# Query weights by head, five late heads, two streaming buffers and seven kept places in a four-layer decoder trunk

## The chip, the cores and the metric

The kernel runs on one core of a Trainium2 chip. The metric is the device time of one execution in microseconds, as the median of several runs. One further execution was taken with the hardware profiler; all views below are of that one.

## The reference, cut to what matters

The program is a decoder trunk of four layers over 256 tokens of 1024 numbers, all in float32. Each layer has a token mixer (HGRN2, FoX attention, Mamba-2 SSD, HGRN2 again) and then a PEER feed-forward: eight heads each choose 16 of 16384 experts for every token, and an expert is one row of a table `u` and one of a table `v`.

```python
for i in range(DEPTH):                      # 4 layers
    hn = rmsnorm(h, norm_mix[i])
    h = h + mixer_i(hn)                     # HGRN2, FoX, SSD, HGRN2
    h = h + peer_ffn(rmsnorm(h, norm_ffn[i]), peer_w_q[i], peer_keys[i], peer_u[i], peer_v[i])
return rmsnorm(h, norm_final)

def peer_ffn(h, w_q, sub_keys, u_tab, v_tab):
    q = (xb @ w_q).reshape(M, 8, 2, 128)                 # w_q: 1024 x 2048
    s = jnp.einsum('mhcd,hckd->mhck', q, sub_keys)       # 2 x 128 scores a head
    sv, si = lax.top_k(s, 16)
    # the 16 x 16 sums of both halves, their top 16, softmax over these: idx, gates
    u, v = u_tab[idx], v_tab[idx]                        # 8 x 16 rows of each a token
    act = gelu(einsum('md,mhkd->mhk', xb, u)) * gates
    return einsum('mhk,mhkd->md', act, v)
```

## The kernel before, in words

**Stages, pairs and gathers.** The 256 tokens are two tiles of 128. A stage is the PEER part of one layer for one tile, so there are eight: stages 0, 2, 4 and 6 (the first, third, fifth and seventh) are first tiles, the others second tiles. A stage has eight heads, a head eight pairs, a pair two gathers. A gather is one indirect DMA on POOL's queue that brings 128 expert rows, u and v side by side, 1 MB in all, into a buffer of the `ring`. For each pair DVE makes two dot products (`dot`), ACT the gate (`active`), PE adds the weighted v rows to `acc` (`spread`, four products of 64x512), and then both buffers go back to the ring. The ring has seven buffers (`GB`), and further 1 MB places are lent to it while they are empty (`given_back`).

**Work beside the pairs.** While stage s is worked off, `side(s)` prepares stage s + 1: its mixer, its norms and its query scores. It is a Python generator; the loop at the end of the program takes one step of it a pair or so, so that a running cost follows `SIDE[s]`, and takes all that is left at pair 62. `Plan` lays out a mixer's work by numbered slots (`pe` for products, `at` for the other engines), and `hold(n, r)` keeps slot n back until r heads are routed. The order on every engine is fixed when the program is built.

**Routing.** `route` takes the scores of one head from `SS` and makes indices (`ix`, the cast from `gs` is its last step on DVE) and gates; heads are routed in order, up to four ahead of the one being gathered. `route_first` makes the very first head's indices in two halves, so that five gathers can go out early.

**Weights.** All weights but the expert tables come as units of 128 x 2048 numbers, 1 MB, on SP's queue. `stream` lists the units in the order of use, and `loads` issues them in `order` as places come free; where the next one has no place, all behind it wait. There are four kinds of places. A streaming buffer (`raw`, `NRAW` of them) is free again when its unit is used. A kept place (`spots`, `NKEPT` of them) holds a mixer unit from the first tile's use to the second's, so that it comes in once for both; `KEEP` gives for each weight the units that have a place, in the places' order. (For FoX one more unit is kept in the mixer's scratch space.) `homes` are other spaces lent to single units of the program's first stretch. `"rest"`, `"x"` and `"keys"` in `order` are other loads, and `"factors"`, `"heads"` and `"states"` are points that must be passed before what follows is loaded.

**Queries.** The query weights of a layer are eight units. Before, two units together held 512 columns, which are two heads. `queries` makes a first tile's heads 0 to 3 at the end of the stage ahead and a second tile's heads 0 to 7: the products are 512 wide (tokens are the stationary side), ACT evicts them to `QB`, PE turns them, ACT copies the turn to `QT`, PE multiplies it with the keys, and ACT copies the scores to `SS`. A first tile's heads 4 to 7 come later, inside its own stage, in the slots of the second tile's mixer (`late_queries`): there the weights are the stationary side and the products, 128 wide, come out turned already. Their units are `tails`, put into the stream behind mixer units by `TAIL`, and kept for the second tile. `alone` makes the program's first two heads one by one.

Of the kernel before, what the change touches and what calls it, by code (L numbers as in the profile page):

```python
# [11 lines left out]
F32 = mybir.dt.float32  # L12
# [19 lines left out]
NRAW = 3  # L32
# [12 lines left out]
SIDE = (47, 31, 43.5, 100, 100, 35.2, 45, 1.8)  # L45
# [55 lines left out]

def _cols(v):
    return np.ascontiguousarray(v.reshape(-1, P).T)
# [12 lines left out]
def _layout(x, norm_mix, norm_ffn, norm_final, hgrn_lb_logits, hgrn_w_in, hgrn_gnorm, hgrn_w_out,  # L116
# [18 lines left out]
    for i in range(DEPTH):  # L135
        a["wq%d" % i] = _in_units(peer_w_q[i])
# [35 lines left out]
def trunk(ctx: ExitStack, tc: tile.TileContext, d: dict, out: bass.AP):  # L172
# [113 lines left out]
    order += range(35, len(stream))  # L286
# [45 lines left out]
    def loads():  # L332

        while order:
# [12 lines left out]
            else:  # L347
# [9 lines left out]
                elif u in homes:  # L357
                    r = homes[u]
                elif pos[0] < NRAW:
                    pos[0] += 1  # L360
                    r = rawp.tile([P, UNIT], F32, name="raw")
                else:
                    return
                if u == 0:
                    for e in (slice(0, HALF), slice(HALF, UNIT)):
                        nc.sync.dma_start(r[:, e], d[nm][i][:, e])
# [4 lines left out]
                raws[u] = r, keep or u in homes  # L371
# [7 lines left out]
    def half(nm, use):  # L379
# [3 lines left out]
        use(raws[u][0].rearrange("p (k c n) -> p k c n", k=2, c=2)[:, k])  # L383
        pos[1] += 1
        if k:
            r, stays = raws.pop(u)
# [170 lines left out]
    def hgrn(l, t, carry):  # L557
# [204 lines left out]
        if t:  # L762
            late_queries(p, l, 4, 9)
# [47 lines left out]
    def fox(l, t, carry):  # L811
# [99 lines left out]
        if t:  # L911
            late_queries(p, l, 4, 9)
# [5 lines left out]
    def ssd(l, t, carry):  # L918
# [228 lines left out]
        if t:  # L1147
            late_queries(p, l, 4, 9)
# [12 lines left out]
    def place_of(s, hh):  # L1161

        return hh if s % 2 or hh not in (4, 5) else hh - 4

    def late_queries(p, l, *starts):

        s = 2 * l
        root = 1.0 if s else rts[1][:, 2:3]
        bs = {}

        def products(g, n):
            if n == 0:
                bs[g] = pjp.tile([P, 512], F32, name="pj")
            ws = [raws[tails[l, 2 * g + i]][0].rearrange("p (k n) -> p k n", k=4) for i in range(2)]
            for k in range(DC):
                mm(bs[g][:, n * P:(n + 1) * P], ws[k // 4][:, k % 4, n * P:(n + 1) * P], xA[:, k], k == 0, k == DC - 1)
            if n == 3:
                for i in range(2):
                    raws.pop(tails[l, 2 * g + i])

        def turned_queries(g):
            return at_["SS"][:, (g - 1) * 512:g * 512].rearrange("p (g t) -> p g t", g=4)

        def evac(g):
            assert routed[0] >= 8 * s + 4, (s, g, routed)
            nc.scalar.copy(turned_queries(g), bs.pop(g).rearrange("p (g t) -> p g t", g=4))

        def score(g):
            b, qt = bank(), turned_queries(g)
            for i in range(4):  # L1190
                mm(b[:, i * P:(i + 1) * P], qt[:, i], keys[:, 4 * g + i], True, True)

            def use():
                h0 = place_of(s, 2 * g)
# [507 lines left out]
```

## Time and profile before

| what | before |
|---|---|
| median of 3 runs | 3159.31 us (3158.54 to 3159.74) |
| profiled execution, time | 3157.22 us |
| profiled execution, span from the first to the last instruction | 3155.5 us |
| busy: PE, DVE, ACT, POOL | 82%, 67%, 49%, 39% |
| moved by DMA | 1292.65 MB, mean 410 GB/s |
| gathers | 1028 DMAs on POOL's queue |
| first gather issued | 109.43 us |

The rows of the profile name an engine, the line of the program (often that of a helper: L249 is any product, L253 a turn, L224 an activation, L211 any DVE operation), the operation and its tiles as out<-in. A float32 product of the program is two rows of PE in the profile, called passes here; a turn is one. In a timeline the first two numbers are the start and the length in us, and what stands in brackets is the idle time ahead and what ended it. In a table of groups the count follows the x, then the busy time in us, the mean ns of one, and the idle time. Most tiles are parts of one large tile, `arena`; `raw`, `pj`, `ps` and `acc` are tiles of their own (`ps` and `pj` are both PSUM banks).

### The profile page before, as it was taken

The numbers are of one execution on the slowest core, as the hardware profiler recorded it, in microseconds if no ns is written. First come the engines' busy times: TensorE is split into PE (matmuls) and PEld (weight loads), VectorE is DVE, ScalarE is ACT, GpSimd is POOL, SyncE is SP. The second block draws the span as 40 slices with busy tenths as digits, with TensorE's granted clock in tenths as the row PEclk, the third lists the DMA queues.
The fourth block names the chain that finished last, engine by engine and source line by source line (L and its number), as shares of the span: only waits on it lengthen the run. The fifth ranks groups of instructions, "written<-read, shape, count | busy, mean of one in ns | idle before, by whom it ended". The sixth has DMA issues, their size and how long they took to land.

```text
span 3155.5 us, 31905 instructions
## 1 busy us (share of the span) xinstructions
PE 2600.9 (82%) x8970; PEld 998.7 (32%) x8970; DVE 2111.5 (67%) x5602; ACT 1546.5 (49%) x4406; POOL 1222.5 (39%) x1034
## 2 busy tenths in 40 slices
PE   9798887787789886999878998778877888876666
PEld 4333332232234432344223443222322333321111
DVE  1666758575666856878476885586656766687755
ACT  3455435374344743577344784355443555344433
POOL 0234434344433533433343333343344433345454
PEclk9999998999899998999989999899989999999999
DMA  8799999999999999999999999999999999999998
GB/s 327 302 421 421 420 421 420 416 401 421 419 414 418 421 421 421 418 400 411 415 421 411 404 419 422 420 419 416 410 414 418 412 421 410 421 421 421 421 421 336
DMA packets 179198, 1292.65 MB, mean 410 GB/s; under 512 B 19920, under 2 KB 20432, under 8 KB 22352
## 3 DMA queue, kind: packets, MB, share of 16 engines
q0 software_dynamic: 147776, 1073.81, 82.4%
q1 hardware_dynamic: 31248, 216.82, 16.7%
q8 instruction: 74, 1.21, 0.2%
q14 instruction: 100, 0.82, 0.1%
HBM read 1289.49 MB, written 1.05 MB: 409 GB/s over the span
## 4 chain that ended last, share of the span: by engine, by line
DMA 52%; DVE 14%; issue 14%; PE 8%; POOL 4%; ACT 2%; POOLq 0%; DVEq 0%; ACTq 0%
DMA arena<-in_uv,ix 52%; DVE arena L211 9%; POOL arena L1462 4%; PE acc L1530 4%; PE pj L249 3%; PE ps L249 2%; DVE eq L211 1%; ACT L224 1%; DVE af L211 1%; ACT dg L224 1%; ACT arena L224 0%; DVE gs L211 0%; DVE si L211 0%; DVE ti L211 0%; PE ps L253 0%
## 5 line engine op out<-in xcount | busy, mean ns | idle before, releaser
L1462 POOL DMA_INDIRECT arena<-in_uv,ix x1028 | 1220.4, 1187 | 1915.9 <-PE acc L1530 1128.6
L211 DVE SCALAR_TENSOR_TENSOR arena<-arena 128x1024 f32<-128x1024 f32 (+3 forms) x1280 | 1317.4, 1048 | 867.4 <-DMA arena<-in_uv,ix 857.6
L1530 PE MATMUL acc<-arena,dg 128*64 128x512 f32 x4096 | 1432.1, 667 | 527.1 <-ACT dg L224 524.5
L224 ACT ACTIVATE dots<-dots 128x1 f32<-128x1 f32 x1024 | 203.6, 199 | 1354.0 <-DVE arena L211 1353.4
L1530 PEld LDWEIGHTS acc<-arena,dg 128*64 128x64 f32 x4096 | 350.3, 145 | 1427.3 <-ACT dg L224 1029.2
L249 PE MATMUL pj<-raw,arena 128*128 128x512 f32 x1184 | 555.1, 610 | 4.9 <-DMA raw<-in_ssm 2.3
L224 ACT ACT_TABLE_LOAD x328 | 420.8, 1283 | 7.6 <-DVE fst L211 1.3
L224 ACT ACTIVATE dg<-dg,dots 128x64 f32<-128x64 f32 x1024 | 356.1, 348 | 33.2
L249 PE MATMUL pj<-arena 128*128 128x512 f32 (+2 forms) x1136 | 347.1, 455 | 4.8 <-ACT arena L976 1.8
L249 PEld LDWEIGHTS pj<-raw,arena 128*128 128x128 f32 x1184 | 215.2, 192 | 343.2 <-issue 320.2
L224 ACT ACTIVATE dg<-m,gs 128x64 f32<-128x64 f32 x1024 | 293.8, 335 | 0.0
L249 PEld LDWEIGHTS pj<-arena 128*128 128x128 f32 x1136 | 174.4, 193 | 181.8 <-issue 163.6
L249 PE MATMUL ps<-arena 128*128 128x128 f32 (+3 forms) x992 | 130.7, 284 | 1.5 <-ACT arena L1260 1.0
L249 PEld LDWEIGHTS ps<-arena 128*128 128x128 f32 (+2 forms) x992 | 100.8, 166 | 66.5 <-issue 38.4
L253 PE MATMUL ps<-fst,arena 128*128 128x128 f32 x536 | 83.9, 282 | 7.2 <-DVE arena L211 4.9
L224 ACT ACTIVATE arena<-arena 128x512 f32<-128x512 f32 (+3 forms) x132 | 67.7, 555 | 43.6 <-DVE arena L211 41.2
L253 PEld LDWEIGHTS ps<-fst,arena 128*128 128x128 f32 x536 | 61.3, 143 | 78.5 <-issue 43.9
L211 DVE DVE_READ_ACCUMULATOR arena<-arena 128x1 f32 x1024 | 84.6, 83 | 0.0
L211 DVE FIND_INDEX8 si<-sv,arena 128x8 uint32<-128x128 f32 x256 | 69.8, 285 | 0.0
L249 PE MATMUL ps<-cst,arena 128*128 128x128 f32 (+3 forms) x288 | 66.6, 358 | 0.1
L211 DVE MAX8 sv<-arena 128x8 f32<-128x128 f32 x256 | 61.6, 282 | 3.5 <-ACT arena L1264 3.4
L224 ACT ACTIVATE arena<-ps 128x512 f32<-128x512 f32 (+4 forms) x120 | 46.7, 435 | 25.4 <-PE ps L249 24.7
(130 smaller groups left out, 1246.1 us busy)
## 6 DMA issues: line engine op xcount, KB each, us to landing
raw<-in_ssm SPq DMA_DIRECT2D x52, 1024.0 KB, 9.5
raw<-in_hg SPq DMA_DIRECT2D x50, 1024.0 KB, 9.5
raw<-in_wq SPq DMA_DIRECT2D x28, 1024.0 KB, 9.4
arena<-in_wq SPq DMA_DIRECT2D x20, 1024.0 KB, 9.2
raw<-in_fox SPq DMA_DIRECT2D x18, 1024.0 KB, 9.2
arena<-in_hg SPq DMA_DIRECT2D x17, 1024.0 KB, 13.4
arena<-in_uv,ix POOLq DMA_INDIRECT x1028, 16.4
arena<-in_fox SPq DMA_DIRECT2D x7, 1024.0 KB, 13.8
```

What stands on the lines that cost most here:

```text
L211: return getattr(nc.vector, name)(o, *a, **k)
L224: nc.scalar.activation(o, i, f, **k)
L249: nc.tensor.matmul(o, w, m, start=start, stop=stop)
L253: nc.tensor.transpose(o, i, ident)
L1462: nc.gpsimd.indirect_dma_start(o, None, src, bass.IndirectOffsetOnAxis(ap=ix, axis=0))
L1530: nc.tensor.matmul(accs[s][e][g * 64:g * 64 + 64], dg[:, g], v, start=hh == 0 and q == 0, stop=hh == 7 and q == NQ - 1)
```

## The change

The query weights are laid out by head: a unit is the 256 columns of one head for all 1024 rows. All query products are made in turned form, 128 wide with the weights stationary, so that no turn is left. A first tile's heads 0 to 2 are made ahead of its stage (`AHEAD_HEADS`), heads 3 to 7 inside it, one in every second slot from slot 2 on. There are two streaming buffers for three, and seven kept places for six. More units of the first stretch have homes, and the orders, holds and two of the pacing numbers are adjusted.

```diff
-NRAW = 3
+NRAW = 2
-KEEP = {"hg": (0, 1, 4, 6, 12, 17), "fox": (0, 1, 4, 6, 9, 13, 11), "ssm": (0, 1, 4, 6, 15, 24), "wq": (4, 5, 6, 7)}
-TAIL = ((6, 4), (6, 5), (8, 6), (9, 7))
-NKEPT = 6
+KEEP = {"hg": (0, 1, 2, 4, 6, 11, 16), "fox": (0, 1, 2, 4, 6, 9, 13, 11), "ssm": (0, 1, 2, 4, 6, 14, 24), "wq": (3, 4, 5, 6, 7)}
+TAIL = ((5, 3), (5, 4), (7, 5), (8, 6), (9, 7))
+AHEAD_HEADS = 3
+NKEPT = 7
-SIDE = (47, 31, 43.5, 100, 100, 35.2, 45, 1.8)
+SIDE = (47, 31, 45, 100, 100, 35.2, 46, 1.8)
+def _head_units(w):
+    k, n = w.shape
+    a = w.reshape(k // P, P, n // 256, 256).transpose(2, 1, 0, 3)
+    return np.ascontiguousarray(a).reshape(n // 256, P, UNIT)
-        a["wq%d" % i] = _in_units(peer_w_q[i])
+        a["wq%d" % i] = _head_units(peer_w_q[i])
-            stream += [("wq%d" % l, i) for i in range(8 if t else 4)]
+            stream += [("wq%d" % l, i) for i in range(8 if t else AHEAD_HEADS)]
-    homes = {4: GB[0], 16: GB[0], 18: GB[1], 19: GB[2], 20: GB[3], 21: GB[4], 22: GB[5], 23: GB[6],
-             26: mix[:, SPACE:SPACE + UNIT], 27: mix[:, D:3 * D], 29: mix[:, 3 * D:5 * D]}
-    order = [0, 1, 2, "rest", *range(3, 10), 22, 10, 11, 12, 23, 13, 14, 15, 16, "x", 17, 20, 18, 21, 19, "keys",
-             "factors", 24, 25, 26, "heads", 27, 28, "states", 29, 30, 33, 34, 31, 32]
+    homes = {3: GB[0], 5: GB[1], 7: GB[2], 8: GB[3], 9: GB[4], 10: at_["XR"], 12: at_["SS"], 15: GB[0], 17: GB[1], 18: GB[2], 19: GB[3], 20: GB[4], 21: GB[5], 22: GB[6],
+             28: mix[:, SPACE:SPACE + UNIT], 26: mix[:, D:3 * D], 32: mix[:, 3 * D:5 * D]}
+    order = [0, 1, 2, "rest", *range(3, 14), 22, 14, 15, 16, 17, "x", 18, 19, 20, 21, "keys",
+             "factors", 23, 24, 25, 28, 27, "heads", 26, 31, "states", 32, 34, 36, 29, 30, 33, 35, 37]
-            late_queries(p, l, 4, 9)
+            late_queries(p, l, (2, 4, 6, 8, 10))
...
+    def free_at(s, hh):
+        if s % 2:
+            return 8 * (s - 1) + (5, 6, 7, 7, 7, 7, 7, 8)[hh]
+        return 8 * s + hh - 2 if hh >= AHEAD_HEADS else 8 * s
+    def head_products(b, ws, x):
+        for n in range(2):
+            for k in range(DC):
+                mm(b[:, n * P:(n + 1) * P], ws[k // 4][:, k % 4, n * P:(n + 1) * P], x[:, k], k == 0, k == DC - 1)
+    def turned_queries(o, b):
+        nc.scalar.copy(o, b[:, 0:256].rearrange("p (c t) -> p c t", c=2))
     def late_queries(p, l, slots):
         s = 2 * l
+        for hh, n in zip(range(AHEAD_HEADS, 8), slots):
+            qt = SS[:, (0, 1, 2, 3, 6)[hh - 3]]
+            def products(hh=hh, qt=qt):
+                b = bank()
+                head_products(b, [r.rearrange("p (c n) -> p c n", n=256) for r in raws.pop(tails[l, hh])[0]], xA)
+                later(lambda: turned_queries(qt, b))
+            p.hold(n, free_at(s, hh))
+            p.pe(n, products)
+            p.pe(n + 1, score, s, hh, qt)
...
+        for n, hh in enumerate(range(0 if s else 2, 8 if s % 2 else AHEAD_HEADS)):
+            p.pe(n, products, hh)
+            p.at(n, lambda hh=hh: turned_queries(QT[hh % 2], bs.pop(hh)))
+            p.hold(n + 1, free_at(s, hh))
+            p.pe(n + 1, score, s, hh, QT[hh % 2])
+        yield from p.run(99)
```

`score` now scales the program's first scores as ACT copies them to `SS`, where the eviction to `QB` did it before; `alone` makes its two heads in the same turned form, into two banks with a copy each.

PE's rows around the program's first score, before (`ps<-fst,arena` 128x128 are turns, 64x128 is the spreading of the first tile's tokens for the dot products):

```order
L249 MATMUL pj<-arena 128x512 x2
L249 MATMUL pj<-arena 128x256 x2
L253 MATMUL ps<-fst,arena 128x128 x4
L249 MATMUL pj<-arena 128x256 x6
L253 MATMUL ps<-fst,arena 128x128 x2
L249 MATMUL ps<-arena 128x128 x2
L249 MATMUL pj<-arena 128x256 x8
L249 MATMUL ps<-fst,arena 64x128 x32
```

And after:

```order
L256 MATMUL pj<-arena 128x512 x2
L256 MATMUL ps<-arena 128x128 x4
L260 MATMUL ps<-fst,arena 128x128 x4
L256 MATMUL ps<-arena 128x128 x30
L256 MATMUL ps<-fst,arena 64x128 x32
L256 MATMUL ps<-arena 128x128 x2
L256 MATMUL pj<-arena 128x128 x16
```

The eight products of 256 columns for each of the first two heads have become sixteen of 128 (the run of 30 is the rest of the first head's, its two score products and the second head's), and the turn of two ahead of the score is gone.

PE's rows in stage 0 at the first late heads, before (`acc<-arena,dg` 64x512 x4 is one pair, `pj<-arena` 128x512 x4 a unit of the second tile's mixer, `pj<-arena` 128x128 the late query products):

```order
L249 MATMUL pj<-arena 128x128 x16
L1530 MATMUL acc<-arena,dg 64x512 x4
L249 MATMUL pj<-arena 128x512 x4
L1530 MATMUL acc<-arena,dg 64x512 x4
L249 MATMUL ps<-cst,arena 128x512 x2
L249 MATMUL pj<-arena 128x128 x8
```

And after, where they are `ps<-arena` 128x128 x16:

```order
L256 MATMUL pj<-arena 128x512 x4
L1528 MATMUL acc<-arena,dg 64x512 x4
L256 MATMUL ps<-arena 128x128 x16
L1528 MATMUL acc<-arena,dg 64x512 x4
L256 MATMUL pj<-arena 128x512 x4
L1528 MATMUL acc<-arena,dg 64x512 x4
L256 MATMUL ps<-arena 128x128 x2
```

The two scores of a late head (the x2) now follow its products after one mixer unit; before, four heads came as two groups, each made over several pairs and scored together.

SP's rows at the end of stage 0, where the second tile's queries and then the next layer's first units are loaded, before:

```order
L368 DMA raw<-in_hg 128x2048 x8
L368 DMA raw<-in_wq 128x2048 x4
L368 DMA arena<-in_fox 128x2048 x2
L368 DMA raw<-in_fox 128x2048 x2
L368 DMA arena<-in_fox 128x2048
```

And after:

```order
L378 DMA raw<-in_hg 128x2048 x8
L378 DMA raw<-in_wq 128x2048 x3
L378 DMA arena<-in_fox 128x2048 x3
L378 DMA raw<-in_fox 128x2048
L378 DMA arena<-in_fox 128x2048
```

One query unit fewer is loaded, since five of the eight are kept, and three of FoX's first four units go to kept places for two.

More of the change, by code (lines that the diff above doesn't have):

```diff
@@ L1161, in place_of @@
     def place_of(s, hh):
-        return hh if s % 2 or hh not in (4, 5) else hh - 4
-    def late_queries(p, l, *starts):
-        s = 2 * l
[L1168 to L1194, printed above, removed]
-                act(SS[:, h0:h0 + 2], b.rearrange("p (h c k) -> p h c k", h=2, c=2), AF.Copy, scale=root)
-                scored.update((s, 2 * g + i) for i in range(2))
-            later(use)
-        for g, n in zip((2, 3), starts):
-            for i in range(4):
-                p.pe(n + i // 2, products, g, i)
-            if g == 2:
-                p.hold(n, 8 * s + 4)
-            p.at(n + 1, evac, g)
-            p.pe(n + 2, score, g)
@@ new lines, in place_of, with score, use @@
+        return hh if s % 2 or hh not in (4, 5, 6) else hh - 4
+    def free_at(s, hh):
+        if s % 2:
+            return 8 * (s - 1) + (5, 6, 7, 7, 7, 7, 7, 8)[hh]
+        return 8 * s + hh - 2 if hh >= AHEAD_HEADS else 8 * s
+    def score(s, hh, qt):
+        assert routed[0] >= free_at(s, hh), (s, hh, routed)
+        b = bank()
+        for c in range(2):
+            mm(b[:, c * P:(c + 1) * P], qt[:, c], keys[:, 2 * hh + c], True, True)
+        def use():
+            act(SS[:, place_of(s, hh)], b[:, 0:256].rearrange("p (c k) -> p c k", c=2), AF.Copy,
+                scale=1.0 if s else rts[1][:, 2:3])
+            scored.add((s, hh))
+        later(use)
@@ L1210, in queries @@
         x = xT if s % 2 else xA
-        ub = {}
+        bs = {}
         top[0] = FREE[KIND[l]]
-        QB = al(512)
-        QT = al(512).rearrange("p (g t) -> p g t", g=4)
-        root = 1.0 if s else rts[1][:, 2:3]
-        def evac(g):
-            act(QB, ub.pop(g), AF.Copy, scale=root)
-        def turns(g):
-            turned(QB, lambda b: nc.scalar.copy(QT, b))
-        def score(g):
-            assert s == 0 or routed[0] >= min(8 * s, 8 * s - 6 + 2 * g + 4 * (s % 2)), (s, g, routed)
-            b = bank()
-            for i in range(4):
-                mm(b[:, i * P:(i + 1) * P], QT[:, i], keys[:, 4 * g + i], True, True)
-            def use():
-                nc.scalar.copy(SS[:, 2 * g:2 * g + 2], b.rearrange("p (h c k) -> p h c k", h=2, c=2))
-                scored.update((s, 2 * g + i) for i in range(2))
-            later(use)
+        QT = [al(256).rearrange("p (c t) -> p c t", c=2) for _ in range(2)]
@@ L1271, in queries @@
         p = Plan()
-        gs = range(0 if s else 1, 4 if s % 2 else 2)
-        p.halves(range(2 * len(gs)), project("wq%d" % l, ub, gs, x))
-        for i, g in enumerate(gs):
-            p.at(2 * i + 1, evac, g)
-            p.pe(2 * i + 2, turns, g)
-            p.pe(2 * i + 3, score, g)
-        for n, _ in enumerate(p.run(99)):
-            yield
-            while n % 2 and s and routed[0] < min(8 * s, 8 * s - 6 + 4 * (s % 2) + len([1 for k in scored if k[0] == s])):
-                yield "wait"
+        for n, hh in enumerate(range(0 if s else 2, 8 if s % 2 else AHEAD_HEADS)):
[4 more added lines that the diff above has]
+        yield from p.run(99)
     def top16(chains):
@@ L1404, in route_first @@
         got[0, 0] = ix, gs
-        while ring[0] is not homes[22]:
+        while ring[0] is not homes[21]:
             fetch(sent[0])
@@ L1601, in trunk @@
         next(first)
+    next(first)
     lone[0] = False
@@ L1608, in trunk @@
         next(first)
+    next(first)
     next(routing)
     next(first)
-    while pos[1] < 2 * 24:
+    while pos[1] < 2 * 23:
         next(first)
```

69 lines of the change are left out of this document (42 added, 27 removed).

## The prediction

> **What bounds the kernel now.** I read the page's summary of engines and slices first, then the queues, then windows along the span, then the waits.
>
> ```profile
> span 3155.5 us, 31905 instructions
> PE 2600.9 (82%) x8970; PEld 998.7 (32%) x8970; DVE 2111.5 (67%) x5602; ACT 1546.5 (49%) x4406; POOL 1222.5 (39%) x1034
> ...
> DMA  8799999999999999999999999999999999999998
> ...
> q0 software_dynamic: 147776, 1073.81, 82.4%
> q1 hardware_dynamic: 31248, 216.82, 16.7%
> ```
>
> No compute engine is full, and the DMA digit is 9 in every one of the 40 slices but the first two and the last. The two queues' shares add up to 99.1% of the 16 engines' span: q0 carries the expert rows (gathers on POOL's queue), q1 the weights (SP's queue). In the window view the last two columns are the DMA share and GB/s:
>
> ```profile
> 0.00:90.00 90.00, 86.73 (x284) 43.12 (x285) 18.75 (x43) 29.00 (x50) 1.16 (x5) 1.00 0.84 335
> 90.00:110.00 20.00, 18.92 (x109) 12.62 (x109) 8.59 (x40) 5.62 (x12) 0.57 (x1) 1.00 0.05 21
> 200.00:300.00 100.00, 91.31 (x376) 41.22 (x376) 62.27 (x161) 54.99 (x147) 40.82 (x33) 0.98 1.01 421
> 1410.00:1420.00 10.00, 10.00 (x39) 3.81 (x38) 9.05 (x31) 3.63 (x11) 4.34 (x3) 1.00 0.80 291
> 1490.00:1500.00 10.00, 10.00 (x33) 4.35 (x33) 9.66 (x20) 5.39 (x16) 2.63 (x3) 1.00 0.85 336
> 1510.00:1530.00 20.00, 20.00 (x57) 6.91 (x55) 4.93 (x8) 3.27 (x13) 5.63 (x6) 1.00 1.01 422
> 1770.00:1780.00 10.00, 10.00 (x49) 6.04 (x49) 8.59 (x32) 9.78 (x27) 3.78 (x4) 1.00 0.90 338
> 120.00:3130.00 3010.00, 2471.72 (x8501) 934.74 (x8501) 2062.46 (x5467) 1496.26 (x4304) 1208.99 (x1019) 0.93 1.01 417
> ```
>
> The program has two parts. Up to about 110 us PE is the bound (86.73 of 90 us busy) and DMA falls idle at the end, 0.05 in 90 to 110. From 120 to 3130 us DMA is the bound: 417 GB/s on average against 421 in an undisturbed window. The difference is (1 - 417/421) x 3010 = 28.6 us of lost transfer, and it lies in dips such as 1410, 1490 and 1770, where PE shows 10.00 of 10 us. One more view agrees: POOL, which issues the gathers, waits for buffers to be released, not for numbers, and a load takes far longer to land than its bytes need:
>
> ```profile
> POOL arena L1462 <- PE acc L1530: 1128.6, 387, 8.7
> ...
> raw<-in_ssm SPq DMA_DIRECT2D x52, 1024.0 KB, 9.5
> raw<-in_wq SPq DMA_DIRECT2D x28, 1024.0 KB, 9.4
> ...
> arena<-in_uv,ix POOLq DMA_INDIRECT x1028, 16.4
> ```
>
> So in the second part a byte not moved is worth its transfer time: one unit of 1,048,576 bytes at 421 GB/s is **2.49 us**. (q1's own row gives 0.167 x 3155.5 / 216.82 MB, or 2.55 us for a unit.)
>
> **Part 1: fewer unit loads.** Counting the load rows of both programs, 199 units come in before (148 into streaming buffers, the rest into kept places and lent space) and 191 after: in each of four layers one more mixer unit is kept, the first tile's queries at the stage's end load three units for four, the late ones five for four, the second tile's three for four. What counts is which are behind the first gather.
>
> ```profile
> 73.79 49.23 SPq L368 DMA_DIRECT2D arena<-in_hg  x3
> 123.07 0.90 SPq L368 DMA_DIRECT2D raw<-in_hg  x2
> 109.43 1.09 POOL L1462 DMA_INDIRECT arena<-in_uv,ix  x1 [107.74 <-DVE ix L211]
> ```
>
> The load list blocks at "states", which is freed after the first gathers (the third load of the merged row is that one, at 123 us). Ahead of it stand 24 units of the first tile and two of the second, 26 in all; in the changed list 23 and two, 25. So 173 follow before and 166 after: **seven** units are saved where DMA is the bound, 7 x 2.49 = **17.4 us** (17.9 by q1's row). The eighth is saved where DMA has idle time, and counts nothing; if PE waited for loads there, it would be a gain too, but PE's 86.73 of 90 excludes more than 3 us.
>
> **Part 2: the first route.** The second part begins when the first gather is issued, so PE's path up to the first score counts in full.
>
> ```profile
> 98.94 2.94 PE L249 MATMUL pj<-arena 128*128 128x256 f32 x12
> 101.92 0.47 ACT L224 ACTIVATE arena<-pj,rts 128x256 f32<-128x256 f32 x1 [1.69 <-PE pj L249]
> 102.44 0.44 PE L253 MATMUL ps<-fst,arena 128*128 128x128 f32 x2 [0.56 <-ACT arena L224]
> 102.97 0.37 ACT L1260 COPY arena<-ps 128x256 f32<-128x256 f32 x1 [0.58 <-PE ps L253]
> 103.40 0.71 PE L249 MATMUL ps<-arena 128*128 128x128 f32 x4 [0.52 <-ACT arena L1260]
> 201.90 3.84 PE L249 MATMUL pj<-arena 128*128 128x128 f32 x32
> ...
> L892 ACT COPY arena<-ps 128x128 f32<-128x128 f32 x16 | 4.0, 248 | 0.0
> L249 PE MATMUL pj<-arena 128*128 128x512 f32 x592 | 277.2, 612 | 4.8 <-ACT arena L976 1.8 <-DVE arena L211 1.4 <-DMA arena<-in_hg 0.9
> L249 PE MATMUL pj<-arena 128*128 128x128 f32 x512 | 62.5, 278 | 0.0
> ```
>
> Before: products, one eviction of 0.47 us, a turn, a copy, then the score at 103.40. After: products, two copies of 128x128 (2 x 0.25 us), then the score: the stretch from 102.44 to 103.40, 0.96 us, goes. The products themselves are 32 passes 128 wide for 16 passes 256 wide: by the row at 201.90 (32 such passes, the late queries before) 3.84 us, against 16/12 x 2.94 = 3.92 us. Bounds: 1.04 us of gain (0.96 and the 0.08 of the passes); none, if the hand-overs between the two copies and the score cost what the turn did. I take **0.9 us**. Loads cannot delay this path: the first 15 units have a place that waits for no other unit, where three streaming buffers were refilled after use, so they only come earlier.
>
> **Part 3: queries in turned form, later on.** A head costs 32 passes 128 wide, 32 x 62.5/512 = 3.91 us, for 8 passes 512 wide, 8 x 277.2/592 = 3.75 us, less two turns (0.44 by the row at 102.44). 48 heads change their form, 12 a layer: from 48 x (3.91 - 3.75 - 0.44), 13 us less of PE, to 48 x 0.16, 8 us more, if the turns hid. PE is 82% busy beside a full DMA, which covers it: **0**; without that cover it would be these 13 or 8 us, and both ends stay in the range. ACT's evictions per head become two of 256 columns; ACT is 49% busy: nothing.
>
> **Part 4: five late heads for four.** In the order, the fourth head of a first tile is routed (its index cast on DVE) after 17 pairs of its stage in the first and third stages, 14 and 16 in the fifth and seventh, and first needed for pair 24: a lead of 7 pairs at the least. Before, the fifth head of the first stage was routed after 25 pairs for pair 32, also 7 (only the program's second head leads by less, 3 pairs in both). In time that was, from the cast to the first gather,
>
> ```profile
> 267.18 0.17 DVE L211 CAST ix<-gs 128x16 int32<-128x16 f32 x1
> 290.62 0.17 DVE L211 CAST ix<-gs 128x16 int32<-128x16 f32 x1
> 295.12 0.94 POOL L1462 DMA_INDIRECT arena<-in_uv,ix  x1 [0.31 <-PE ps L249]
> ```
>
> 28 us (267.18 to 295.12). The queue of gathers does not run dry for it: 0. The new holds in the late slots wait for heads that are routed by then; the old one at 8s + 4 goes.
>
> **Part 5: two streaming buffers.** A unit's load now waits for the unit two before it, not three. Where units come 10 us and more apart that is harmless. The tightest place is the Mamba output projection at the end of a stage:
>
> ```profile
> 1509.17 1.95 PE L249 MATMUL pj<-raw,arena 128*128 128x512 f32 x4 [0.85 <-DMA raw<-in_ssm]
> 1518.27 1.94 PE L1530 MATMUL acc<-arena,dg 128*64 128x512 f32 x8
> 1520.13 3.70 PE L249 MATMUL pj<-raw,arena 128*128 128x512 f32 x8
> 1525.63 3.70 PE L249 MATMUL pj<-raw,arena 128*128 128x512 f32 x8
> ```
>
> There PE takes a unit each 5.5 us (1520.13 to 1525.63: a unit 3.70, a pair 1.94). With two buffers a buffer's cycle is 9.5 us to land and 3.7 to use, 13.2 us for two units, 6.6 each: 1.1 us late for each of about seven units, twice, 15 us; and in each of seven bursts of query units the third is issued 2 x 5.5 - 3.7 = 7.3 us before its use and lands after 9.4, 2.1 us late, 15 us again. That is 30 us of PE waiting, if all of it showed. But a pair with its unit needs 3 x 2.49 = 7.5 us of DMA, more than 6.6: DMA is the bound in these bursts too (0.85 of wait already shows while 1510 to 1530 runs at 422 GB/s), and seven gather buffers hold 17.4 us. Bounds: 0 and 30 us; I take **0**, nearest the row of 422, and let a rival take more.
>
> **Sum.** 17.4 + 0.9 = 18.3 us. The profiled execution took 3157.2 us (span 3155.5), so 3138.9; it stood 2.1 us under the median of the runs, 3159.3, so **3141 us**.
>
> **The rivals.** (a) The dips grow: PE's work stays while DMA's shrinks, and the two-buffer waits fall where PE is already full (1410, 1490, 1770). A fifth to two fifths of part 5's 30 us comes back: 3147 to 3153. For it: three dips lie in the Mamba stages. Against: the 422 GB/s in the burst itself.
> (b) The dips shrink: the late heads stand on alternate slots, not on neighbouring ones (1770 is such a place), and one head leaves the forced end of three stages. A sixth to a third of 28.6 us: 3131 to 3136.
> (c) Slower: the fourth head's route comes late, since its unit lands in a place that the stage's first unit frees two slots earlier. The 28 us of lead must go first, then 18.3 + 6.3 us over four stages, 6.2 each: it decides from 34 us on. A slip of two routes, 23.4 us each from the cast at 267.18 to the next, would cost 4 x (46.8 - 28) = 75 us: 3216. Against: every lead in the order is 7 pairs or more.
> (d) Slower: a 128-wide pass waits for its own weight load. The load's row is
>
> ```profile
> L249 PEld LDWEIGHTS pj<-raw,arena 128*128 128x128 f32 x1184 | 215.2, 192 | 343.2 <-issue 320.2
> ```
>
> 192 ns; not hidden, a pass would take 0.122 + 0.192 = 0.314 us, a head 10.0, a pair with it 12.0 us against DMA's 7.5. It decides from 5.6 us a head on. 41 heads in bursts (11 a layer, less three ahead of the gathers) x 4.5 = 185 us, less seven bursts' cover of 17.4: 3204. Against: the row of 62.5 us for 512 such passes has the loads in it.
> The Trainium skill, "TensorE: Matmul & The Clock Gate", section "Back-to-back issue gap", speaks for (d): it says that a stream of weight load and matmul pairs is paced by both, about 81 ns at 128 columns and 131 at 512. By that ratio a head would cost 4 x 81/131 = 2.5 times as much, an estimate of 9.3 us. The trace disagrees for this kernel's float32 passes: 0.122 against 0.469 us, a ratio of 3.8 for four times the columns.
> (e) The change does not do what it says: excluded for the loads, which are rows of the program; only their place could differ, and then the time would be the same within what a measurement can tell, 0.2% or 6.3 us.
>
> **Chances.** Forecast, 3136 to 3146: 0.62. (a) 0.18, a third of it not faster by 0.2%. (b) 0.11. (c) 0.04. (d) 0.03. (e) 0.02. Faster by over 0.2% (under 3153): 0.62 + 0.11 + 0.12 = 0.85; within: 0.06 + 0.02 = 0.08; slower: 0.07. The range takes in (b) and most of (a): 3130 to 3152.
>
> **What the changed profile would show.** Part 1: q1 down from 216.82 by 8.4 to 208.4 MB, q0 as it was, and 120 to 3110 us again near 417 GB/s. Part 2: the first gather near 108.5 us. Part 3: about 0.12 us a pass in the 128-wide rows. Part 4: gaps on POOL waiting for the index cast would show it wrong. Part 5: PE waiting for raw rises from a few us to some 20, without a fall of GB/s at the ends of the Mamba stages; lower GB/s there is (a). I am wrong if the mean of 417 falls by more than 1 GB/s.

## The result, and the profile after

The changed kernel takes **3141.07 us** (median of four runs, 3137.26 to 3144.13) against 3159.52 us (3158.54 to 3159.88) before on the same chip: a ratio of 0.9941, 95% interval 0.9924 to 0.9959, or 18.45 us less. The forecast was 3141.0. Its profiled execution took 3143.29 us, 2.2 us over its median, where that of before stood 2.3 us under its own; so the two traces differ by 14 us only, and a second profiled execution of the changed kernel (below) is read beside the first.

The page of the changed kernel: span, engines, the slices' DMA digits, the two queues, and two rows of the tables.

```profile
span 3141.5 us, 34004 instructions
PE 2593.9 (83%) x10010; PEld 1094.9 (35%) x10010; DVE 2111.1 (67%) x5602; ACT 1544.5 (49%) x4449; POOL 1224.8 (39%) x1034
...
DMA  8699999999999999999999999999999999999998
...
q0 software_dynamic: 147776, 1073.81, 82.7%
q1 hardware_dynamic: 30096, 208.43, 16.1%
```

q0 is what it was; q1 is down from 216.82 to 208.43 MB, eight units of 1.0486 MB. The engines' work is the same to a part in two hundred, but for PE's weight loads (PEld, 1094.9 us for 998.7). DMA is still full from the third slice on.

Windows of the changed kernel (start:end and length, busy time and rows of PE, PEld, DVE, ACT and POOL, granted clock, DMA share, GB/s): the whole second part, the stretches in which before had its dips of 1410 and 1770, the two Mamba output projections, and the fourth, fifth and sixth stages. A stage begins 8 or 9 us earlier than before, so the stretches of the dips are 8 us earlier too.

```profile
120.00:3110.00 2990.00, 2461.15 (x9489) 1025.23 (x9488) 2059.92 (x5462) 1493.28 (x4341) 1209.27 (x1017) 0.93 1.01 416
1378.00:1418.00 40.00, 37.61 (x137) 15.75 (x136) 32.52 (x99) 30.58 (x75) 11.93 (x10) 1.00 0.99 405
1757.00:1787.00 30.00, 26.54 (x120) 14.08 (x121) 25.50 (x79) 23.27 (x60) 11.38 (x10) 1.00 1.01 421
1480.00:1540.00 60.00, 48.82 (x136) 17.95 (x134) 30.07 (x58) 22.58 (x66) 17.58 (x16) 0.91 0.90 351
1910.00:1960.00 50.00, 42.20 (x118) 15.53 (x117) 21.76 (x40) 14.46 (x47) 11.19 (x12) 0.90 0.97 388
1226.00:1636.00 410.00, 342.41 (x1246) 139.95 (x1246) 303.71 (x838) 241.93 (x641) 151.44 (x128) 0.93 0.99 408
1636.00:2057.00 421.00, 373.11 (x1621) 183.77 (x1622) 295.65 (x796) 235.55 (x642) 151.71 (x128) 0.94 1.01 416
2057.00:2427.00 370.00, 302.35 (x1020) 108.42 (x1018) 255.15 (x658) 180.13 (x521) 148.41 (x130) 0.92 1.01 419
```

The same stretches of before that the prediction did not show:

```profile
1386.00:1426.00 40.00, 39.19 (x151) 17.65 (x150) 32.59 (x98) 30.92 (x78) 15.08 (x11) 1.00 0.95 382
1765.00:1795.00 30.00, 28.37 (x139) 15.89 (x139) 28.35 (x85) 26.25 (x62) 10.43 (x9) 1.00 0.97 379
1480.00:1540.00 60.00, 50.94 (x154) 18.67 (x154) 34.40 (x75) 22.84 (x65) 16.24 (x16) 0.98 0.98 402
1910.00:1960.00 50.00, 42.22 (x109) 13.31 (x109) 23.30 (x48) 19.26 (x58) 14.99 (x15) 0.90 1.01 421
1235.00:1644.00 409.00, 349.04 (x1195) 135.91 (x1194) 300.90 (x828) 239.95 (x639) 153.22 (x128) 0.95 1.00 413
1644.00:2062.00 418.00, 370.58 (x1404) 161.21 (x1402) 294.48 (x801) 233.54 (x622) 150.43 (x129) 0.94 1.01 416
2062.00:2440.00 378.00, 303.96 (x972) 104.63 (x970) 251.65 (x636) 179.97 (x520) 154.18 (x129) 0.92 1.01 415
```

The mean of the second part is 416 GB/s, where it was 417. But it is made up otherwise. The dip around 1410 is smaller (405 GB/s over its 40 us for 382), that around 1770 is gone from its 30 us (421 for 379). The two Mamba output projections, 1480 to 1540 and 1910 to 1960, fell from 402 to 351 and from 421 to 388. The sixth stage rose from 415 to 419. The engines' totals tell nothing of this, the GB/s by stage do; so the experiments are read by one measure: **lost transfer**, (1 - GB/s / 421.5) x length of a stage, with the GB/s unrounded and 421.5 as the undisturbed rate. For the fourth stage it is (1 - 408/421.5) x 410, or 13 us, after, and (1 - 413/421.5) x 409, or 8 us, before. "All eight" in the table is 120 to 3110 us. The measure is good to some 3 us in the sum: where two executions differ by it, their spans agree with it to that much in most cases (one is 4.5 us off).

### The profile page after: what moved, and what is told of

Its sections match the earlier page's. It is cut to its first block, busy times and chain, and to the rows that moved or that the text cites. A ratio compares the mean times of both kernels' runs of the same rounds, so it can differ in the third digit from the quotient of the medians.

```text
span 3141.5 us, 34004 instructions
## 1 busy us (share of the span) xinstructions
PE 2593.9 (83%) x10010; PEld 1094.9 (35%) x10010; DVE 2111.1 (67%) x5602; ACT 1544.5 (49%) x4449; POOL 1224.8 (39%) x1034
## 3 DMA queue, kind: packets, MB, share of 16 engines
q1 hardware_dynamic: 30096, 208.43, 16.1%
## 4 chain that ended last, share of the span: by engine, by line
DMA 48%; issue 15%; PE 13%; DVE 10%; POOL 5%; ACT 3%; POOLq 0%; DVEq 0%
DMA arena<-in_uv,ix 46%; DVE arena L218 7%; PE acc L1528 5%; POOL arena L1460 5%; PE pj L256 5%; PE ps L256 3%; DMA raw<-in_ssm 1%; ACT L231 1%; DVE eq L218 1%; ACT dg L231 1%; DVE af L218 1%; ACT arena L231 1%; PE ps L260 0%; DVE gs L218 0%; DMA raw<-in_wq 0%
## 5 line engine op out<-in xcount | busy, mean ns | idle before, releaser
L256 PE MATMUL pj<-raw,arena 128*128 128x512 f32 x832 | 400.5, 623 | 26.4 <-DMA raw<-in_ssm 22.9
L231 ACT ACTIVATE dg<-dg,dots 128x64 f32<-128x64 f32 x1024 | 356.1, 348 | 33.2
L256 PE MATMUL pj<-arena 128*128 128x128 f32 (+1 forms) x1248 | 344.3, 428 | 2.1 <-DVE arena L218 1.0
L256 PEld LDWEIGHTS pj<-raw,arena 128*128 128x128 f32 x832 | 154.0, 196 | 272.0 <-issue 234.2
L256 PE MATMUL ps<-arena 128*128 128x128 f32 (+5 forms) x1696 | 224.9, 284 | 4.3 <-ACT arena L1267 4.3
L256 PEld LDWEIGHTS ps<-arena 128*128 128x128 f32 (+3 forms) x1696 | 184.7, 177 | 106.2 <-issue 58.4
L256 PE MATMUL pj<-arena,raw 128*128 128x128 f32 x672 | 81.3, 280 | 4.9 <-DMA raw<-in_wq 4.9
L231 ACT ACTIVATE arena<-ps 128x256 f32<-128x256 f32 (+3 forms) x170 | 63.9, 407 | 41.8 <-PE ps L256 41.1
L256 PEld LDWEIGHTS pj<-arena,raw 128*128 128x128 f32 x672 | 78.6, 196 | 11.3 <-DVE arena L218 5.7
L260 PE MATMUL ps<-fst,arena 128*128 128x128 f32 x440 | 69.8, 286 | 2.4 <-DVE arena L218 2.2
```

Of the source, the lines that this page charges most:

```text
L231: nc.scalar.activation(o, i, f, **k)
L256: nc.tensor.matmul(o, w, m, start=start, stop=stop)
L260: nc.tensor.transpose(o, i, ident)
```

## Experiments

Every kernel was timed against the kernel before on the same chip, in turns, and profiled once. Their lost transfer, in us:

| kernel | 4th stage | 5th | 6th | 4th to 6th | all eight | first gather at |
|---|---|---|---|---|---|---|
| before | 8.0 | 5.9 | 5.4 | 19.3 | 32.6 | 109.43 |
| changed | 13.4 | 5.4 | 2.3 | 21.1 | 36.6 | 107.69 |
| changed, second time | 12.2 | 5.5 | 2.0 | 19.7 | 32.6 | 107.38 |
| three streaming buffers, six kept | 7.4 | 4.5 | 6.0 | 17.9 | 30.1 | 108.46 |
| old queries, two and seven | 13.4 | 4.1 | 3.2 | 20.7 | 33.2 | 108.78 |
| six units loaded twice | 11.7 | 5.6 | 1.7 | 19.0 | 32.1 | 108.83 |
| units 26 and 28 kept | 6.0 | 8.5 | 2.7 | 17.2 | 30.7 | 108.61 |
| units 14 and 28 kept | 6.4 | 10.3 | 2.3 | 19.0 | 32.6 | 107.80 |
| seventh place not lent | 11.8 | 7.0 | 2.4 | 21.2 | 36.2 | 108.12 |
| 26 and 28 kept, late heads spread | 6.9 | 7.1 | 5.7 | 19.7 | 33.2 | 107.79 |
| three and seven, ring of six | 7.0 | 9.1 | 6.1 | 22.2 | 44.1 | 107.73 |
| query products twice | 11.1 | 28.9 | 2.9 | 42.9 | 72.9 | 108.21 |
| late heads late | 6.2 | 7.2 | 1.7 | 15.1 | 45.2 | 107.33 |

**The two halves of the change, each alone.** First the new layout and the five late heads with the old buffers; 170 units follow the first gather.

```diff
 # on the changed kernel
-NRAW = 2
+NRAW = 3
-KEEP = {"hg": (0, 1, 2, 4, 6, 11, 16), "fox": (0, 1, 2, 4, 6, 9, 13, 11), "ssm": (0, 1, 2, 4, 6, 14, 24), ...}
+KEEP = {"hg": (0, 1, 2, 4, 6, 11), "fox": (0, 1, 2, 4, 6, 9, 11), "ssm": (0, 1, 2, 4, 6, 14), ...}
-NKEPT = 7
+NKEPT = 6
```

> The changed kernel with three streaming buffers and six kept places, as before the change: only the query layout, the late heads and the first stretch's homes are left of it. 170 units follow the first gather, 166 in the changed kernel, 173 before. Theory 1 (a unit costs its transfer, 2.49 us, and two buffers cost some 8 us of starved DMA at the ends of the Mamba stages, which better spread query work elsewhere gave back): 3141 + 4 x 2.49 - 8, about 3143 us, and the loss of transfer between 1480 and 1540 us falls from 10 us to under 4. Theory 2 (units only; the waits for two buffers are hidden and the dips are chance): 3151 us, and the dip at 1480 to 1540 stays.

Then the old queries with the new buffers, also 170 units.

```diff
 # on the kernel before
-NRAW = 3
+NRAW = 2
-KEEP = {"hg": (0, 1, 4, 6, 12, 17), "fox": (0, 1, 4, 6, 9, 13, 11), "ssm": (0, 1, 4, 6, 15, 24), ...}
+KEEP = {"hg": (0, 1, 4, 6, 11, 16, 2), "fox": (0, 1, 4, 6, 9, 13, 2, 11), "ssm": (0, 1, 4, 6, 14, 24, 2), ...}
-NKEPT = 6
+NKEPT = 7
```

> The kernel before with two streaming buffers and seven kept places (the further kept unit is number 2 of HGRN2, FoX and Mamba each), with the old query layout and order. 170 units follow the first gather for 173. Theory 1: 3159.5 - 3 x 2.49 + 8, about 3160 us, no gain, with waits for streaming buffers at the ends of the Mamba stages and GB/s falling there. Theory 2: 3152 us. In both the first gather may be up to 2 us later, since the first stretch streams through two buffers.

Measured: 3146.53 us, 0.9974 [0.9964, 0.9985], 8.1 us less; and 3148.66 us, 0.9981 [0.9972, 0.9990], 6.0 us less. Each saves three units, 3 x 2.49 = 7.5 us; the first has the new start as well. Together 14.1 us, and with the one unit that only both save, 2.5, it is 16.6, against 18.45 and 17.3 in two measurements of the whole. So the halves add up, and units account for nearly all of it: what the two buffers take away in the fourth stage (7.4 lost with three, 13.4 with two, with either form of queries) does not show in the time as the 8 us that the first theory wanted. Both times are near the second theory's (some 8 us less for each), not the first's (16 less and none); the waits and the burst are as the first had them.

The waits of PE's products for the Mamba units in the streaming buffers (sum in us, count, and the longest) in the first and in the second of these kernels:

```profile
PE pj L256 <- DMA raw<-in_ssm: 0.9, 1, 0.9
```

```profile
PE pj L249 <- DMA raw<-in_ssm: 25.6, 14, 4.9
```

The wait belongs to the number of buffers, not to the layout. The window of the burst in these two kernels says the same in GB/s, 421 and 363:

```profile
1480.00:1540.00 60.00, 51.33 (x140) 18.12 (x140) 31.74 (x67) 22.33 (x64) 15.49 (x15) 0.93 1.01 421
```

```profile
1480.00:1540.00 60.00, 51.26 (x154) 19.69 (x154) 33.29 (x69) 23.73 (x68) 17.56 (x17) 0.94 0.95 363
```

**Six units loaded again.** Kept units 5 and 6 of the places' order are loaded a second time in the three layers that are not Mamba's; all else stays.

```diff
-                elif not keep or (nm, i) not in kept:
+                elif not keep or (nm, i) not in kept or (nm[:3] != "ssm" and k in (5, 6)):
```

> The changed kernel, which loads the units of kept places 6 and 7 (counted from 1) again for the second tile in both HGRN2 layers and in FoX: six further units behind the first gather, into the places that hold the same numbers, nothing else. Both theories: 6 x 2.49 = 14.9 us more, 3156 us, and DMA at the same GB/s. A rival (DMA has room in those layers, and the gain came from elsewhere): less than half of it, under 3148 us.

Measured: 3153.62 us, 0.9994 [0.9985, 1.0003]. Six units more, in the row of its queue,

```profile
q1 hardware_dynamic: 30960, 214.72, 16.5%
```

6.29 MB, cost 14.2 us (0.9994 - 0.9949, of 3157) or 16.7 (0.9994 - 0.9941), by which measurement of the changed kernel is taken: 2.4 to 2.8 us each, with lost transfer unchanged (32.1). The intervals leave some 5 us either way in the sum. Nearly the whole gain of the change is gone again. This is the price of a byte, taken by itself.

**The kept places moved into the burst.** Instead of Mamba units 14 and 24, two from inside the eight of its output projection are kept (24 is the first of these); the number of loads is the same.

```diff
-"ssm": (0, 1, 2, 4, 6, 14, 24)
+"ssm": (0, 1, 2, 4, 6, 26, 28)
```

> The changed kernel with two of Mamba's seven kept units moved: 26 and 28 for 14 and 24, so that the eight units of the output projection are not streamed one behind the other. Bytes, buffers and queries as in the changed kernel. Theory 1: the waits of PE for a streamed Mamba unit (22.9 us in the changed kernel, 9 waits) fall by more than half, the loss at 1480 to 1540 falls from 10 to under 4 us, and the time falls by 5 to 8 us, to about 3134 us. Theory 2: no change, 3141 us.

Measured: 3136.70 us, 0.9941 [0.9927, 0.9954]. Its waits, and its windows of the burst, the fourth stage, the fifth, and 100 us inside the fifth:

```profile
PE pj L256 <- DMA raw<-in_ssm: 9.0, 9, 2.0
```

```profile
1480.00:1540.00 60.00, 50.31 (x142) 17.45 (x141) 32.20 (x64) 22.94 (x71) 17.67 (x17) 0.94 1.01 417
1225.00:1630.00 405.00, 337.13 (x1246) 136.63 (x1246) 304.10 (x838) 241.41 (x642) 151.37 (x128) 0.96 1.01 415
1630.00:2052.00 422.00, 375.03 (x1621) 182.59 (x1622) 295.72 (x796) 235.67 (x641) 150.01 (x128) 0.93 1.00 413
1690.00:1790.00 100.00, 92.03 (x396) 47.56 (x396) 78.56 (x255) 59.15 (x160) 31.00 (x28) 0.95 0.98 394
```

The burst was mended, as meant: PE's wait is 9.0 us, the burst runs at 417 GB/s for 351, and the fourth stage is 405 us long for 410. But the fifth stage is 422 for 421, and falls to 394 GB/s between 1690 and 1790, where the changed kernel had 417. By the ratio there is nothing in it.

**Is it the unit that is no longer kept?** One of the two is put back: 14 kept, 28 for 24.

```diff
-"ssm": (0, 1, 2, 4, 6, 14, 24)
+"ssm": (0, 1, 2, 4, 6, 14, 28)
```

> The changed kernel with Mamba's kept unit 28 for 24: unit 14 stays kept in the middle of the convolution's units, and 28 stands in the middle of the output projection's eight. Theory (each lost transfer in the Mamba stages comes from PE waiting for a streamed unit, and a kept unit breaks the row of them where it stands): lost in the fourth stage 7 to 9 us for 13.4, in the fifth 5 as in the changed kernel, not 8.5 as with 26 and 28 kept; 3 to 6 us faster than the changed kernel on the same chip. Rival (what is lost in one place is won in another): the same time within 2 us.

It ran beside a second measurement of the changed kernel, unaltered:

> The changed kernel once more, unaltered, beside the kernel before on one chip, as the ruler for the runs of this chip. By the first four kernels (the sum of what six kept places with the new layout and seven with the old one gave, and one unit more) 0.994 to 0.995 of before; transfer lost in the fourth stage (pairs of the second FoX tile, with Mamba's first tile beside them) 11 to 14 us as in all kernels with two streaming buffers and the units 14 and 24 kept, against 7 to 8 with three.

Measured: 3138.55 us, 0.9942 [0.9928, 0.9955], and for the unaltered one 3139.76 us, 0.9949 [0.9936, 0.9963]. Both are the same to what can be told. The fifth stage and its middle in the kernel with 14 and 28:

```profile
1633.00:2053.00 420.00, 372.07 (x1619) 182.91 (x1616) 293.08 (x792) 233.56 (x632) 149.39 (x127) 0.95 1.00 411
1690.00:1790.00 100.00, 92.18 (x395) 47.41 (x394) 78.81 (x256) 59.27 (x161) 30.49 (x28) 0.95 0.98 396
```

396 GB/s between 1690 and 1790 again, though 14 is kept. So it is not the load of that unit that costs there, and in neither kernel does PE wait for a streamed unit in that window. What both share is that the fourth stage lost less, and also that 28 is kept and 24 is not; no run separates the two. A smaller loss in the fourth stage does not by itself bring a larger one in the fifth: with three streaming buffers and six kept places they were 7.4 and 4.5.

**PE's cover, taken away in part.** Every head's query products are made twice into the same bank (but for the program's first two heads); the numbers that come out are the same.

```diff
     def head_products(b, ws, x):
-        for n in range(2):
+        for n in (0, 1, 0, 1):
```

> The changed kernel with every query product made twice (the second time over the first, with the same numbers): 32 passes of 128 columns more a head, 64 x 3.91 = 250 us of PE work more, no bytes and no waits added by hand. If PE's work is covered by the DMA as the prediction's third part has it: the pair with a head's products takes 1.94 + 7.8 = 9.8 us of PE against 7.5 of DMA, and what exceeds is smaller than the gather buffers' cover, so 0 to 10 us more. If PE is as near to being the bound as DMA: 40 to 100 us more. The first gather comes 3.9 us later in both, for the first head's own products.

Measured: 3173.90 us, 1.0050 [1.0035, 1.0066]: 34 us more than the changed kernel, between the two forecasts. The first gather is at 108.21 us and not 3.9 us later, since the first two heads have products of their own that the edit does not reach. Its second part, its fourth and its fifth stage:

```profile
120.00:3140.00 3020.00, 2587.82 (x11423) 1233.41 (x11421) 2056.00 (x5453) 1487.35 (x4340) 1176.41 (x1017) 0.95 1.00 411
1221.00:1644.00 423.00, 366.61 (x1543) 170.76 (x1542) 305.85 (x864) 240.42 (x643) 142.10 (x128) 0.96 1.00 410
1644.00:2089.00 445.00, 405.10 (x2037) 226.85 (x2038) 295.19 (x796) 234.30 (x642) 149.06 (x129) 0.98 0.97 394
```

1934 passes more (11423 - 9489), 236 us at 0.122, and a seventh of that is in the time. Of the 40 us more of lost transfer 23 lie in the fifth stage, which is 405 of 445 us busy on PE. PE's free time of 530 us in the second part is therefore not one cover. In the fifth stage 416 passes more (2037 - 1621) are 51 us, and nearly half of that is lost there; in the fourth 297 more (1543 - 1246) are 36 us, and the lost transfer does not rise (11.1 for 12.2 and 13.4).

**The lead of the late heads, taken away.** They stand in neighbouring slots, the fourth head five slots later.

```diff
-            late_queries(p, l, (2, 4, 6, 8, 10))
+            late_queries(p, l, (7, 8, 9, 10, 11))
```

> The changed kernel with the five late heads in slots 7 to 11 of the mixer instead of 2, 4, 6, 8 and 10. The fourth head is then routed after 24, 23, 19 and 23 pairs of the first, third, fifth and seventh stages, for pair 24. By the prediction's rule (7 pairs of lead were 28 us, a pair is 5.9 us): 13, 7.5, 0 and 7.5 us short, 28 us more in all. Rival (the gathers that are under way, 16 us to landing, cover a late route as well): under 6 us more.

Measured: 3148.34 us, 0.9972 [0.9961, 0.9983], 8.6 us more than the changed kernel, between the forecast and the rival. The fourth head's index cast in the first stage (its row in DVE's timeline) is at 259.49 us, and its first gather is the second row here, 0.9 us later, on POOL:

```profile
259.49 0.17 DVE L218 CAST ix<-gs 128x16 int32<-128x16 f32 x1
```

```profile
245.22 0.94 POOL L1460 DMA_INDIRECT arena<-in_uv,ix  x1 [2.99 <-DVE arena L218]
260.42 0.94 POOL L1460 DMA_INDIRECT arena<-in_uv,ix  x1 [14.27 <-PE acc L1528]
```

No lead at all in the first, third and seventh stages, POOL idle for 14.27 us (put down to the pair that came last, though the index was there only just before); in the third and seventh the gaps are 8.88 and 7.77 us. Together they make 30.9 us, near the 28 that were worked out, and yet they cost 8.6. In its own stage a gap costs more than half of itself, as the first stage shows, 411 GB/s where the changed kernel has 421:

```profile
123.00:498.00 375.00, 308.70 (x1258) 138.02 (x1258) 249.30 (x676) 173.34 (x504) 136.11 (x121) 0.92 0.99 411
```

That is (421 - 411)/421.5 x 375 = 8.9 us for 14.27; the gathers in flight, up to seven of 2.49 us, can go on meanwhile. The four stages whose lead was taken away lose some 20 us more together than in the second measurement of the changed kernel, but the other four lose some 10 less, the fourth alone 6 (6.2 for 12.2). Why they do stays open.

**Why does the sixth stage lose 2 us and not 5?** The seventh kept place is empty there and is lent to the ring. It isn't lent:

```diff
-        if k in wanted:
-            wanted.remove(k)
+        if k in wanted or k == 6:
+            wanted.discard(k)
```

> The changed kernel, but the seventh kept place is not lent to the ring of gather buffers while it is empty; nothing else. Theory (the seventh place is also a further gather buffer from a layer's last use of its unit to the next layer's load, and that is why the sixth stage loses 2 us of transfer with seven kept places, against 5.4 and 6.0 with six): the sixth stage loses 5 to 6 us again and the time is 2 to 5 us above the changed kernel's 0.9949 of before, about 0.996. Rival (the sixth stage's difference has another cause, such as the shorter row of streamed units): no change, 0.9949.

Measured: 3141.91 us, 0.9952 [0.9939, 0.9966]. The sixth stage stays as it was in the changed kernel, 419 GB/s:

```profile
2057.00:2425.00 368.00, 296.36 (x1017) 107.67 (x1017) 253.53 (x655) 179.68 (x519) 146.82 (x130) 0.93 1.01 419
```

So the lent place is not the reason.

**A streaming buffer for a gather buffer.** Three streaming buffers and seven kept places, with a ring of six.

```diff
-NGB = 7
+NGB = 6
-NRAW = 2
+NRAW = 3
-    homes = {3: GB[0], ..., 21: GB[5], 22: GB[6],
+    homes = {3: GB[0], ..., 21: GB[5],
```

> The changed kernel with three streaming buffers, seven kept places and six gather buffers instead of two, seven and seven (query unit 2 of the first stretch goes to a streaming buffer). Bytes and queries as in the changed kernel. If the streamed units' lateness is the main loss: the fourth stage loses 6 to 8 us for 12 to 13, and the time is 3 to 5 us below the changed kernel's. If the cover of seven gather buffers is worth more than a streaming buffer: losses rise in every stage, and the time is 5 to 15 us above it.

Measured: 3147.53 us, 0.9964 [0.9951, 0.9978]. The fourth stage lost 7.0 us for 12, as with three buffers before, but all eight together 44.1, some 14 to 17 us more in the others. By lost transfer the gather buffer is worth more; in time it is 5 to 7 us, and the interval overlaps those of the changed kernel ([0.9936, 0.9963] and [0.9924, 0.9959]).

**Kept in the burst, and the late heads spread.** Were the fifth stage's loss due to the late heads standing close, this would take it away.

```diff
-"ssm": (0, 1, 2, 4, 6, 14, 24)
+"ssm": (0, 1, 2, 4, 6, 26, 28)
...
-            late_queries(p, l, (2, 4, 6, 8, 10))   # Mamba's second tile
+            late_queries(p, l, (2, 5, 8, 11, 14))
```

> The changed kernel with Mamba's kept units 26 and 28 for 14 and 24, and with Mamba's late heads in slots 2, 5, 8, 11 and 14, where they meet fewer of its input units. Theory (in the fifth stage PE is full from 1690 to 1790 and is the bound there; what the kept units save at the end of the fourth stage is lost there): the fifth stage loses 5 us, not 8.5, the fourth 6, and the time is 5 us below the changed kernel's, about 0.9935 of before. Rival: PE's work of the whole fifth stage counts, not its place: lost again 8 or 9 us there, 0.994.

Measured: 3139.67 us, 0.9940 [0.9927, 0.9954]. The fifth stage loses 7.1 us (8.5 when not spread, 5.5 in the changed kernel), between the two forecasts, and the sixth now 5.7; the time is the rival's. What was won in the fifth was lost one stage on, as far as differences of this size can be told.

## Why the prediction was right, point by point

**Part 1 held.** q1 moved 208.43 MB, the forecast's 208.4. Seven units at 2.49 us are 17.4 us; the six units loaded again cost 2.4 to 2.8 us each, and the halves of the change give about three units' worth each.

**Part 2 held in its mechanism.** The first stretch of PE up to the score, in the timeline of the changed kernel:

```profile
82.21 3.70 PE L256 MATMUL pj<-arena 128*128 128x512 f32 x8 [0.67 <-ACT arena L726]
...
101.23 0.27 ACT L1267 COPY arena<-ps 128x128 f32<-128x128 f32 x1 [1.58 <-PE ps L256]
101.40 0.27 ACT L1268 COPY arena<-ps 128x128 f32<-128x128 f32 x1
101.55 4.29 PE L256 MATMUL ps<-arena 128*128 128x128 f32 x36 [0.19 <-ACT arena L1267]
...
107.69 1.08 POOL L1460 DMA_INDIRECT arena<-in_uv,ix  x1 [106.00 <-DVE ix L218]
```

The score starts 0.32 us after the first of the two copies starts, with no turn between. The first gather goes out at 107.69 us for 109.43, 1.74 earlier, where 0.9 was forecast. But part of that is an earlier start of everything. Counted from the same row in both, PE's after its idle 0.67 us, it is 25.48 us for 26.65, that row in before being

```profile
82.78 3.70 PE L249 MATMUL pj<-arena 128*128 128x512 f32 x8 [0.67 <-ACT arena L715]
```

Five executions with the new queries (the changed kernel twice, three of the experiments) have 25.47 or 25.48, and the two with the old ones 26.65 and 26.02: the gain is 0.5 to 1.2 us, inside the bounds of 0 and 1.04 but for the top, which one execution of before makes. The other 0.57 us varies by execution (the row stands at 81.90 to 83.36 in those five) and is no gain.

**Part 3 held for the price, not for the reason given.** The rows of the query products:

```profile
L256 PE MATMUL pj<-arena,raw 128*128 128x128 f32 x672 | 81.3, 280 | 4.9 <-DMA raw<-in_wq 4.9
L256 PE MATMUL pj<-arena 128*128 128x128 f32 x672 | 80.3, 279 | 0.0
```

81.3/672 is 0.121 us a pass, so rival (d) is out. The Trainium skill's rule ("TensorE: Matmul & The Clock Gate", "Back-to-back issue gap": pairs of load and product paced by both, 81 ns at 128 columns for 131 at 512) is not borne out for these float32 passes: 0.121 us here against 3.70/8 = 0.462 for 512 columns, as the column count has it. "PE is 82% busy beside a full DMA, which covers it" is too broad: 236 us of added passes cost 34 us, 23 of the 40 us of lost transfer in one stage. The change's own -13 to +8 us of PE would have been worth up to 2 us at that rate, an estimate, so 0 was near enough.

**Part 4 held**: with the order as it is, the casts lead as forecast, in the first stage by 26.9 us:

```profile
218.40 0.17 DVE L218 CAST ix<-gs 128x16 int32<-128x16 f32 x1
245.31 0.94 POOL L1460 DMA_INDIRECT arena<-in_uv,ix  x1 [0.30 <-issue]
```

Rival (c)'s rule, that each us by which the lead falls short counts in full, is an upper bound: without the lead the time rose by 8.6 us, not the 28 that this rule made of it.

**Part 5 is the step that failed at its place.** "DMA is the bound in these bursts too" is wrong for the two Mamba output projections. The changed kernel's PE there, and its waits for streamed units (sum, count, longest):

```profile
1492.82 1.94 PE L1528 MATMUL acc<-arena,dg 128*64 128x512 f32 x8
...
1499.32 7.95 PE L256 MATMUL pj<-raw,arena 128*128 128x512 f32 x12 [4.56 <-DMA raw<-in_ssm]
...
1521.37 5.37 PE L256 MATMUL pj<-raw,arena 128*128 128x512 f32 x8 [4.33 <-DMA raw<-in_ssm]
```

```profile
PE pj L256 <- DMA raw<-in_ssm: 22.9, 9, 4.6
PE pj L256 <- DMA raw<-in_wq: 4.9, 5, 1.9
```

A unit's load takes 9.8 us to land (9.5 before), the last number of its row:

```profile
raw<-in_ssm SPq DMA_DIRECT2D x50, 1024.0 KB, 9.8
```

PE waits for 22.9 us for Mamba's units (2.3 before) and for 4.9 for the queries': the sum of 28 is near the upper bound of 30 us, but otherwise divided (Mamba's units were put at 15, the queries' at 15), and it falls on fewer units, up to 4.6 us each where 1.1 was worked out. While PE waits, the pairs behind it wait too, their buffers don't come back, and the gathers stop: 351 GB/s in 1480 to 1540 costs (402 - 351)/421.5 x 60 = 7.3 us, 1910 to 1960 another (421 - 388)/421.5 x 50 = 3.9. That is rival (a) as described, and with three buffers or with units kept in the burst it goes away (421 and 417 GB/s), which shows the cause.

The total is right nevertheless, because other losses shrank beside it, as rival (b) had it in its sum: the two dips by (405 - 382)/421.5 x 40 + (421 - 379)/421.5 x 30 = 5.2 us, and the sixth stage loses 2.0 to 2.3 us for 5.4. But (b)'s reasons, the late heads on alternate slots and one head fewer at the forced end, are not what it takes. The first dip lies in a second tile's stage, which has no late heads. And each half of the change alone has smaller losses in the same places of its stages: the old queries and late heads with two streaming buffers (394 and 421 GB/s), and the new ones with three (413 and 412):

```profile
1383.00:1423.00 40.00, 36.70 (x134) 15.68 (x134) 32.55 (x99) 30.59 (x75) 12.87 (x11) 1.00 0.97 394
1763.00:1793.00 30.00, 27.17 (x121) 14.30 (x121) 28.13 (x92) 28.56 (x70) 12.83 (x10) 1.00 1.01 421
1388.00:1428.00 40.00, 39.77 (x151) 17.45 (x148) 30.99 (x95) 31.87 (x81) 16.70 (x13) 1.00 1.01 413
1756.00:1786.00 30.00, 26.71 (x120) 14.08 (x119) 24.59 (x77) 23.17 (x61) 10.17 (x10) 0.94 1.01 412
```

In the sixth stage the former loses 3.2 us and the latter 6.0. What shrank the dips stays open; both halves keep Mamba's units 2 and 14, which the kernel before does not, and no run tests that by itself. The forecast's sum held neither the loss nor the gain; that they nearly cancel is luck. A like balance is found in other orders, though: in all kernels but the two with work or waits added on purpose, the fourth to sixth stages together lose 17 to 22 us, however that is split. What isn't lost in the burst is mostly lost in the fifth stage or the sixth. The nearest reading is that in these stages PE and DMA are nearly equal in their work (PE 373 of 421 us busy in the fifth), so that a stall of the gathers lets PE run ahead with its own work, and time saved from a stall is met by PE's work later; the doubled products, which put 23 us more into the fifth stage, speak for it. It is argued, not shown. **What stays open** is why the sixth stage loses 2 us in most kernels with two streaming buffers and 5 to 6 with three and in one with two; the lent place is excluded.

**The sum.** From the first trace to the second the span fell by 14.0 us: 17.4 of units, 1.74 of start, less 4.0 of more lost transfer, makes 15.1. In the second execution of the changed kernel lost transfer was 32.6, as before, and the span 3137.1: 18.4 less, where 17.4 and 2.05 make 19.5. So the terms close to 1.1 us in both. The 17.4 us of units are what the forecast said; the start gave 1.74 and 2.05 us for 0.9, of which 0.5 to 1.2 are the queries'; and the 0 of part 5 was a loss in the bursts met by gains elsewhere. That the median meets the forecast to 0.1 us is luck: executions of the changed kernel spread over 7 us, and its second measurement was 17.3 us less than before, not 18.45. The mean of 416 to 417 GB/s stayed within its bound of 1.

## What to carry to other kernels

Where a queue of transfers is full, price a saved load at its bytes by the sustained rate, and count only the loads that are issued after the point where the transfers become the bound. When a resource is halved in number (here a buffer), compare the time in which a load lands with the pace of its use, stage by stage: the mean rate of the program hides a stall that its own window shows. And before mending such a stall, ask whether another engine is as full in the same stretch: three ways of mending this one brought nothing that can be told (0.9940 to 0.9942, for 0.9941 and 0.9949), as the loss came back a stage or two later.

## What the runs showed of the hardware that was not expected

The same kernel differs by 4.9 us between chips or sessions (before: medians of 3154.61 to 3159.52), so only ratios on the same chip were used here; and executions of the changed kernel spread over 7 us (3137.26 to 3144.13), those of before over 1.3 in the same series. Gaps of 14.27, 8.88 and 7.77 us in the issue of gathers cost the program 8.6 us in all. And one streaming buffer of 1 MB did not pay for one gather buffer of the same size, 0.9964 for 0.9949 and 0.9941, though it took away a visible wait (22.9 us of PE waiting for Mamba's units against 1.1).
